# A third weight pair's first products at three seams, and TensorE orders that alternate row halves, in a two-layer decoder trunk

## The chip, the cores and the metric

The kernel runs on one core of a Trainium2 chip. The metric is device time in microseconds of one launch; the time before is the median of three runs, 2896.13 us (2890.81 to 2898.02). A core has five engines with an instruction queue each: TensorE (PE, matmuls into PSUM; its weight loads are listed as PEld), VectorE (DVE), ScalarE (ACT), GpSimd (POOL) and SyncE (SP, here the queue that issues most transfers).

## The reference

Two layers on a sequence of 1024 tokens of width 1024, in float32. Each layer adds three normed branches to the residual: a token mixer, cross-attention into 256 memory tokens, and an MLP with a squared ReLU:

```python
x = x + rms_norm(t, g[1])            # t: RG-LRU block in layer 0, RWKV-7 in layer 1
c = mem_cross_attention(rms_norm(x, g[2]), mem_n, c_w_q[i], c_w_kv[i], c_w_o[i])
x = x + rms_norm(c, g[3])
m = sqrelu_mlp(rms_norm(x, g[4]), m_w_up[i], m_w_down[i])
x = x + rms_norm(m, g[5])
```

RWKV-7 has 16 heads of 64 and a state of 64 x 64 per head:

```python
w_log = -softplus(-(w0 + tanh(xw @ w1) @ w2)) - 0.5        # decay, from a width of 64
a = sigmoid(a0 + (xa @ a1) @ a2)                           # also from a width of 64
state = state * w_t + (state a_t) b_t^T + v_t k_t^T        # per token and head
y_t = state r_t
bonus = sum(r * k * r_k, per head) * v
out = ((group_norm(y) + bonus) * g) @ w_o
```

## The kernel before, in words

**Products in three parts.** A float32 product is made of three fp32r matmuls: `split` (lines 228 to 235) gives a tile's rounded high part (a cast on ScalarE, L233) and the rest (a subtraction on VectorE, L234), and `mm3` (L314 to L320) issues high x high, high x low and low x high. A plain fp32 matmul, where it is used, shows as two records. Activations are stored transposed, 128 rows of the width by 512 tokens.

**Who sets the order.** The program is written once in Python; a planner with a model of the engines then puts the instructions of each engine in order. It takes the earliest written instruction that its model holds to be ready, so TensorE's order can differ from the written one. Tiles come from pools: 45 buffers of 4 KB per partition (`u`), and PSUM's 8 banks in two pools. `bank(n)` takes a bank from pool n. Two tools fix orders: `line(name)` puts each engine's instructions of a block behind the ones that the last block of that name gave to that engine, and `behind()` puts them behind the last instruction written so far. Weights come through a list recorded in a dry run: `fetch` loads entries ahead (`depth + ahead`), `advance` splits the next `depth` of them.

**The 7-product projections** (`cphase`, lines 466 to 563). A projection takes its weights in pairs of 128 columns, counted from 0, and makes each pair with seven half-size products (p1 to p7) in place of eight. A product is four steps of `mm3`, so 12 matmuls. p1 and p2 (in `begin`) need the activations' quarters b11 and b21, both from the first 512 tokens. p5, p6, p7 and p4 need t1 to t4, sums of quarters, and p3 needs b22; these come from the second 512 tokens, which `combine_in` (lines 373 to 432) transposes on TensorE (L386), scales (L389 on VectorE, L391 on ScalarE), subtracts (L417) and splits. `combine_w` forms a pair's weight sums on GpSimd.

**The seams.** Before a projection stands `tphase`, an output projection over eight tiles of 128 tokens; `tail` norms each tile (L655 to L663), stores the residual (L657) and loads the old one (L636). Three projections are begun while the one before still runs: the query projection of layer 1 behind RWKV and both MLP up-projections. There `make` (L454), called after token tiles 4 and 5, loads, splits and combines pairs 0 and 1. At the seam `together` begins both pairs (p1, p2 of pair 0, p1 of pair 1, then the second half's transposes, then p2 of pair 1), and goes on with p5, p6, p7, p3, p4 for both. Pair 2 comes after them: its `begin` is also what fetches its weights and those of the pairs behind it. The order of p1, p2 and the transposes on TensorE is the planner's.

**RWKV.** `decay(f)` (L1297) makes two tiles of 128 x 1024, the decay and the gate a, from operands of 64 rows: rows 0 to 63 for one, 64 to 127 for the other, each in two halves of 512 tokens, one after the other. `evac_v` (L1526) finishes the value projection for tile f: centring products (L1545), the bonus sum as an fp32 product with a matrix of ones (L1562), the gate product; then stores. The scan (L1737 to L1821) runs over 16 chunks of 64 tokens. Its steps stand in a list `todo`, each in `line("scan")`, so every engine runs them in the written order. `values`, `from_state`, `solved`, `update` and `output` are the recurrence for chunk c; `scan_gram` (L1644) makes chunk c+1's grams for half of the heads per call, 8 fp32 matmuls of 64 rows that alternate in the text between the row halves; `scan_keys` transposes keys, `scan_mask` masks grams; `flip_out` (L1698) transposes the finished chunk c-2 (L1703), multiplies on VectorE (L1708) and adds on GpSimd (L1709). `load` brings a pair of chunks' operands through SP.

Of the kernel before, what the change touches and what calls it, by code (L numbers as in the profile page):

```python
# [20 lines left out]
UP = (2, 2)  # L21
# [28 lines left out]
class Net:  # L50
# [322 lines left out]
    def combine_in(self, xs, hf, g, B):  # L373
# [4 lines left out]
        def turned(ks):  # L378
            for k in ks:
                if k % 2 == 0:  # L380
                    t = raw[hf, k // 2] = self.unit()
                    pair = [self.bank(1) for _ in range(2)] if hf else self.halves()
                o = slice((k % 2) * 512, (k % 2) * 512 + 512)
                p = pair[k % 2]
                for i, x in enumerate(xs):
                    nc.tensor.transpose(p[:, i * 128:i * 128 + 128], x[:, k * 128:k * 128 + 128], self.ident)  # L386
                gc = self.colt[:, g + k:g + k + 1]
                if k in (1, 3):
                    nc.vector.tensor_scalar(t[:, o], p, gc, None, ALU.mult)  # L389
                else:  # L390
                    nc.scalar.activation(t[:, o], p, AF.Copy, scale=gc)  # L391
# [62 lines left out]
    def make(self, w, i):  # L454

        self.depth, self.ahead = 0, 2 - 2 * i
        two, first = self.take(("w", w, i))
        self.made[i] = two, first, self.combine_w(two, first)
# [7 lines left out]
    def cphase(self, w, n, B, func, evac, then=None, ahead=2):  # L466
# [4 lines left out]


        place = lambda i: 0 if i < ahead else (i + 1) % 2

        def begin(i, mid=lambda: None):
            two, first = self.made[i][:2] if i in self.made else self.take(("w", w, i))
            h, l = first
            x, z = self.bank(place(i)), self.bank(place(i))
            c0, c1 = self.unit(), self.unit()
            self.product(x, (h[:, a], l[:, a]), B["b11"], True, False)  # L480
            nc.scalar.copy(c0[:, a], x)
            mid()
            self.product(z, (h[:, b], l[:, b]), B["b21"], True, True)
            nc.vector.tensor_add(c0[:, a], c0[:, a], z)
            st[i] = x, c0, c1, two, first
# [44 lines left out]

        def together(two, mid=lambda: None, late=lambda: None):
            for i in two:
                narrow(i)
                begin(i, mid if i == two[-1] else lambda: None)
                finish(i)
                if then and i == n - 2:
                    then[0]()
            late()
            for step in (p5, p6, p7, p3, p4):
                for i in two:  # L540
                    step(*st[i], i)
# [9 lines left out]

        together(range(ahead), second_half)
        for i in range(ahead, n - 2 if then else n):
            narrow(i)
            begin(i)
            finish(i)
            rest()
# [579 lines left out]
def rwkv_consts(self):  # L1137
# [37 lines left out]
    for h in range(2):  # L1175
        nc.gpsimd.memset(self.ones[h * 64:h * 64 + 64, h * 64:h * 64 + 64], 1.0)

    self.center = c([128, 128], "center")
    nc.vector.scalar_tensor_tensor(self.center, self.ones, -1.0 / 64, self.ident, ALU.mult, ALU.add)
# [61 lines left out]
def rwkv(self, X, xt, lw_wa, lw_g, post, mid):  # L1241
# [55 lines left out]
    def decay(f):  # L1297
        cs = slice(f * 128, f * 128 + 128)
        c1 = lambda t: t[:, f:f + 1]
        lw, a = self.unit(), self.unit()  # L1300
        for t, r, b in ((lw, slice(0, 64), self.w0h), (a, slice(64, 128), self.a0h)):
            for hf in range(2):
                s = slice(hf * 512, hf * 512 + 512)
                p = self.bank()
                self.mm3(p, (wa2[0][r, cs], wa2[1][r, cs]), (hwa[0][r, s], hwa[1][r, s]), True, True)
                nc.scalar.activation(t[:, s], p, AF.Tanh, bias=c1(b), scale=0.5)
# [219 lines left out]
    def evac_v(f, p):  # L1526
# [8 lines left out]
        pr, kp = ld.pop(f)  # L1535
        nc.vector.scalar_tensor_tensor(pr, pr, self.col("r_k", f), kp, ALU.mult, ALU.mult)


# [20 lines left out]
        for e in range(2):  # L1559
            s = slice(e * 512, e * 512 + 512)  # L1560
            bp = self.bank()
            mm(bp, self.ones, pr[:, s], start=True, stop=True)  # L1562
            nc.vector.tensor_mul(vt[:, s], vt[:, s], bp)
# [80 lines left out]
    def scan_gram(c, g):  # L1644
# [5 lines left out]
        for q in range(4):  # L1650
            for h in range(2):
                mm(s["pv", g][h][:, q, :], s["st"][g][hr[h], q].rearrange("p w t -> p (w t)"), s["mv"][hr[h], 4 * g + q],  # L1652
                   start=True, stop=True)

# [82 lines left out]
    for c in range(16):  # L1737
# [58 lines left out]
        if c:  # L1796
            todo += [(scan_scale, c + 1)]
        todo += [(values, 0), (from_state, 0)]
        if c > 1:
            todo += [(flip_out, c - 2)]  # L1800
        todo += [(values, 1), (from_state, 1)]
        if c:
            todo += [(post_var, c - 1)]
        todo += [(solved, 0), (solved, 1)]
        if c:
            todo += [(scan_gram, c + 1, 0)]
# [29 lines left out]
def network(net, I, out):  # L1836
# [12 lines left out]
    for l in range(2):  # L1849
        if l == 1:  # L1850
            xt = nxt
            post, nxt = net.tail(g(1, 1), x[3], x[4], net.lncol(1, 2), combine=True)
            rwkv(net, raw, xt, *early, post, lambda tt: tt in MAKE and net.make(I["c_w_q"][1], MAKE.index(tt)))
        post, xt = net.tail(g(l, 3), x[3 * l + 1], x[3 * l + 2], net.lncol(l, 4), combine=True)
        net.xattn(l, nxt, post, lambda tt: tt in MAKE and net.make(I["m_w_up"][l], MAKE.index(tt)))
        raw = []
# [26 lines left out]
```

## Time and profile before

| | us |
|---|---|
| median of 3 runs | 2896.13 (2890.81 to 2898.02) |
| the profiled execution | 2897.32 |
| its span | 2895.6 |
| TensorE busy | 2804.9 (97%) |
| VectorE busy | 1834.2 (63%) |
| ScalarE busy | 1421.7 (49%) |
| GpSimd busy | 907.3 (31%) |

The three seams lie near 690, 2043 and 2277 us of the span, the decays between 1359 and 1463, the value projections from 1636 to 1765, the scan from 1764 to 1935. Busy time of TensorE is read with care: matmuls overlap, one record covers about 0.39 us while the next starts 0.23 us after it, so a stretch can show 5.00 of 5 us busy and still be at half pace; the number of instructions in a stretch and the granted clock (PEclk) tell. In a timeline the first two columns are start and duration in us, equal neighbours are merged (x16), and the bracket gives idle time of the engine before and what ended it. In the stretches each engine has busy us and a count. In the list of waits stand total, times and the longest.

### The profile page before, as it was taken

How to read it: one execution, taken by the hardware profiler on the slowest of the kernel's cores; microseconds unless marked ns; L12 is line 12 of the kernel's file. 1: busy time of each engine (PE TensorE's matmuls, PEld its weight loads, DVE VectorE, ACT ScalarE, POOL GpSimd, SP SyncE). 2: the span in 40 equal slices, each digit the busy share in tenths (PEclk: the TensorE clock that was granted, in tenths of full speed). 3: DMA queues.
4: the chain of work that ended last, by engine and by line, in shares of the span. 5: the costliest groups of instructions: out<-in, count | busy, mean ns of one | idle time of the engine just before them, and what ended most of it. 6: DMA issues, size and time to landing. Idle time of an engine off the chain costs nothing.

```text
span 2895.6 us, 42717 instructions
## 1 busy us (share of the span) xinstructions
PE 2804.9 (97%) x16955; PEld 2341.9 (81%) x16955; DVE 1834.2 (63%) x1995; ACT 1421.7 (49%) x2195; POOL 907.3 (31%) x962
## 2 busy tenths in 40 slices
PE   7999999999999999999999999999999999999998
PEld 6888788887888888887877777888788788888886
DVE  5577566657455577886675724775665645567778
ACT  5455354546454543347561634564463645454333
POOL 2000114023666500012288113753202276650001
PEclk9999999999999999999999999999999999999999
DMA  8212342323444654442657898952232354464443
GB/s 260 73 50 74 109 161 74 111 80 96 154 148 156 224 183 155 151 136 83 172 142 210 224 231 237 231 146 88 88 95 73 109 163 154 138 243 162 151 175 116
DMA packets 383592, 421.92 MB, mean 146 GB/s; under 512 B 91184, under 2 KB 294176, under 8 KB 383392
## 3 DMA queue, kind: packets, MB, share of 16 engines
q1 hardware_dynamic: 371360, 379.19, 43.5%
q0 software_dynamic: 11568, 39.41, 3.8%
q8 instruction: 133, 2.18, 0.3%
q14 instruction: 67, 0.55, 0.1%
q10 hardware_dynamic: 464, 0.59, 0.1%
HBM read 283.79 MB, written 134.74 MB: 145 GB/s over the span
## 4 chain that ended last, share of the span: by engine, by line
PE 86%; DVE 5%; ACT 3%; DMA 2%; issue 2%; SPq 1%; POOL 0%; DVEq 0%; POOLq 0%; ACTq 0%
PE q L318 17%; PE q L320 17%; PE q L319 17%; PE p L318 9%; PE p L320 9%; PE p L319 9%; DVE u L234 1%; PE q L1652 1%; ACT u L233 1%; PE q L386 1%; DMA u<-in_b_w_rkv 1%; DVE u L1199 1%; PE q L1545 1%; PE q L1769 1%; ACT u L930 1%
## 5 line engine op out<-in xcount | busy, mean ns | idle before, releaser
L234 DVE TENSOR_TENSOR u<-u,u 128x1024 fp32r<-128x1024 f32 (+1 forms) x594 | 799.3, 1378 | 353.9 <-ACT u L233 331.8
L233 ACT CAST u<-u 128x1024 fp32r<-128x1024 f32 (+1 forms) x594 | 582.2, 1019 | 416.3 <-DVE u L1042 224.7
L318 PE MATMUL q<-u,u 128*128 128x512 f32 (+2 forms) x1984 | 760.3, 386 | 15.4 <-ACT u L391 10.0
L319 PE MATMUL q<-u,u 128*128 128x512 f32 (+2 forms) x1984 | 759.6, 384 | 0.5 <-POOL u L366 0.5
L320 PE MATMUL q<-u,u 128*128 128x512 f32 (+2 forms) x1984 | 753.9, 384 | 0.8 <-DVE u L234 0.8
L318 PE MATMUL p<-u,u 128*128 128x512 f32 (+1 forms) x1472 | 557.0, 381 | 12.2 <-ACT u L233 5.4
L319 PE MATMUL p<-u,u 128*128 128x512 f32 (+1 forms) x1472 | 553.1, 376 | 3.7 <-DVE u L234 3.6
L320 PE MATMUL p<-u,u 128*128 128x512 f32 (+1 forms) x1472 | 552.6, 376 | 3.6 <-DVE u L234 3.6
L318 PEld LDWEIGHTS q<-u,u 128*128 128x128 f32 (+1 forms) x1984 | 373.6, 189 | 92.8 <-ACT u L391 10.9
L320 PEld LDWEIGHTS q<-u,u 128*128 128x128 f32 (+1 forms) x1984 | 373.9, 189 | 74.3 <-DVE u L234 1.0
L329 POOL TENSOR_SCALAR s<-s 128x1 f32<-128x1 f32 x98 | 39.0, 398 | 1258.3 <-ACT u L327 1256.7
L319 PEld LDWEIGHTS q<-u,u 128*128 128x128 f32 (+1 forms) x1984 | 374.2, 189 | 72.3 <-POOL u L366 1.0
L318 PEld LDWEIGHTS p<-u,u 128*128 128x128 f32 x1472 | 281.2, 191 | 66.4 <-ACT u L233 7.5
L319 PEld LDWEIGHTS p<-u,u 128*128 128x128 f32 x1472 | 281.3, 191 | 55.0 <-DVE u L234 6.7
L320 PEld LDWEIGHTS p<-u,u 128*128 128x128 f32 x1472 | 281.3, 191 | 54.7 <-DVE u L234 5.2
L440 POOL TENSOR_TENSOR u<-u,u 128x512 f32<-128x512 f32 x120 | 189.1, 1579 | 9.0 <-PE q L319 5.1
L1100 DVE TENSOR_TENSOR z<-z,q 128x512 f32<-128x512 f32 x192 | 130.5, 683 | 81.0 <-PE q L320 81.0
L318 PE MATMUL q<-z,u 128*128 128x512 f32 x320 | 124.7, 391 | 1.6 <-ACT u L233 1.6
L320 PE MATMUL q<-z,u 128*128 128x512 f32 x320 | 124.5, 390 | 1.1 <-DVE u L234 1.1
L319 PE MATMUL q<-z,u 128*128 128x512 f32 x320 | 124.6, 389 | 0.0
L441 POOL TENSOR_TENSOR u<-u 128x512 f32<-128x512 f32 x40 | 70.0, 1749 | 166.1 <-DVE u L234 63.7
L997 POOL TENSOR_TENSOR u<-u,u 128x512 f32<-128x512 f32 x32 | 44.2, 1381 | 177.0 <-ACT u L986 159.8
(247 smaller groups left out, 3334.6 us busy)
## 6 DMA issues: line engine op xcount, KB each, us to landing
u<-d SPq DMA_DIRECT2D x194, 512.0 KB, 4.7
d<-u SPq DMA_DIRECT2D x109, 512.0 KB, 3.5
d<-u POOLq DMA_DIRECT2D x68, 512.0 KB, 3.3
d<-u SPq DMA_DIRECT2D x132, 256.0 KB, 3.6
u<-in_m_w_up SPq DMA_DIRECT2D x64, 512.0 KB, 5.5
u<-in_m_w_down SPq DMA_DIRECT2D x64, 512.0 KB, 8.1
u<-in_c_w_kv SPq DMA_DIRECT2D x32, 512.0 KB, 6.5
u<-in_b_w_rkv SPq DMA_DIRECT2D x24, 512.0 KB, 6.2
```

The costliest lines, as they stand in the source:

```text
L233: self.nc.scalar.copy(hv, src)
L234: (eng or self.nc.vector).tensor_tensor(lv, src, hv, ALU.subtract)
L318: mm(o, ah, bh, start=first, stop=False, **kw)
L319: mm(o, ah, bl, start=False, stop=False, **kw)
L320: mm(o, al, bh, start=False, stop=last, **kw)
L329: nc.gpsimd.tensor_scalar(v, ss, 1.0 / n, eps, ALU.mult, ALU.add)
L386: nc.tensor.transpose(p[:, i * 128:i * 128 + 128], x[:, k * 128:k * 128 + 128], self.ident)
L440: sub = lambda o, x, y: nc.gpsimd.tensor_tensor(o, x, y, ALU.subtract)
L441: nc.gpsimd.tensor_tensor(s[:, a], f1[:, a], f1[:, b], ALU.add)
L930: nc.scalar.activation(e[:, s], p[:, s], AF.Exp, bias=mx[:, i:i + 1], scale=1.0 / 16.0, accum_out=sm[:, i:i + 1])
L997: tt(s1, r21, r22, ALU.add)
L1100: nc.vector.tensor_add(to_, to_, o)
```

## The change

- `make` is called from token tile 4 on. For tiles 4 and 5 it looks ahead by two in both cases, so that tile 5 also asks for pair 2's weights; for tiles 6 and 7 it splits them.
- At the three seams pair 2's `begin` (p1, p2) moves into `together`, ahead of p5, and its `combine_w` ahead of p7. The transposes of the second half and p1, p2 of the three pairs form the line "seam": TensorE runs them in the written order. Where no pair was made early (the query projection of layer 0), nothing changes.
- `decay` takes both tiles' matmuls for a half of the tokens in turn, row half by row half, into two banks, in the line "decay"; `scan_gram`'s matmuls form the line "gram" inside the scan's.
- The bonus sum takes a split of r x k x r_k and an fp32r matrix of ones: two fp32r matmuls for one fp32 matmul.
- In the scan `flip_out` moves from between the two calls of `values` to behind `solved`.

```diff
@@ combine_in @@
-                for i, x in enumerate(xs):
-                    nc.tensor.transpose(p[:, i * 128:i * 128 + 128], x[:, k * 128:k * 128 + 128], self.ident)
+                with self.line("seam") if hf and self.held is None else ExitStack():
+                    for i, x in enumerate(xs):
+                        nc.tensor.transpose(p[:, i * 128:i * 128 + 128], x[:, k * 128:k * 128 + 128], self.ident)
@@ make @@
-        self.depth, self.ahead = 0, 2 - 2 * i
+        if i >= len(MAKE):
+            self.depth, self.ahead = 2, 0
+            self.fetch(self.taken - 1)
+            return
+        self.depth, self.ahead = 0, 2
@@ cphase @@
+        early = ahead if 0 in self.made else None
...
-            self.product(x, (h[:, a], l[:, a]), B["b11"], True, False)
+            seam = lambda: self.line("seam") if early and i <= early else ExitStack()
+            with seam():
+                self.product(x, (h[:, a], l[:, a]), B["b11"], True, False)
             nc.scalar.copy(c0[:, a], x)
             mid()
-            self.product(z, (h[:, b], l[:, b]), B["b21"], True, True)
+            with seam():
+                self.product(z, (h[:, b], l[:, b]), B["b21"], True, True)
...
+            if third:
+                self.depth, self.ahead = 0, 2
+                begin(third)
+                self.depth, self.ahead = UP
             late()
             for step in (p5, p6, p7, p3, p4):
+                if step is p7 and third:
+                    finish(third)
...
-        together(range(ahead), second_half)
+        together(range(ahead), second_half, third=early)
         for i in range(ahead, n - 2 if then else n):
             narrow(i)
-            begin(i)
-            finish(i)
+            if i == early:
+                self.fetch(self.taken - 1)
+            else:
+                begin(i)
+                finish(i)
@@ decay @@
-        for t, r, b in ((lw, slice(0, 64), self.w0h), (a, slice(64, 128), self.a0h)):
-            for hf in range(2):
-                s = slice(hf * 512, hf * 512 + 512)
-                p = self.bank()
-                self.mm3(p, (wa2[0][r, cs], wa2[1][r, cs]), (hwa[0][r, s], hwa[1][r, s]), True, True)
+        for hf in range(2):
+            s = slice(hf * 512, hf * 512 + 512)
+            ps = [self.bank() for _ in range(2)]
+            for n, (i, j) in enumerate(((0, 0), (0, 1), (1, 0))):
+                for p, r in zip(ps, hr):
+                    with self.line("decay"):
+                        mm(p, wa2[i][r, cs], hwa[j][r, s], start=n == 0, stop=n == 2)
+            for t, p, b in zip((lw, a), ps, (self.w0h, self.a0h)):
                 nc.scalar.activation(t[:, s], p, AF.Tanh, bias=c1(b), scale=0.5)
@@ evac_v @@
+        prs = self.split(pr)
...
-            mm(bp, self.ones, pr[:, s], start=True, stop=True)
+            for i in range(2):
+                mm(bp, self.ones_r, prs[i][:, s], start=i == 0, stop=i == 1)
@@ scan @@
-        todo += [(values, 0), (from_state, 0)]
-        if c > 1:
-            todo += [(flip_out, c - 2)]
-        todo += [(values, 1), (from_state, 1)]
+        todo += [(values, 0), (from_state, 0), (values, 1), (from_state, 1)]
         if c:
             todo += [(post_var, c - 1)]
         todo += [(solved, 0), (solved, 1)]
+        if c > 1:
+            todo += [(flip_out, c - 2)]
```

More of the change, by code (lines that the diff above doesn't have):

```diff
@@ L529, in narrow, with together @@
                 self.depth, self.ahead = 2 * (n - 1 - i), 0
-        def together(two, mid=lambda: None, late=lambda: None):
+        def together(two, mid=lambda: None, late=lambda: None, third=None):
             for i in two:
@@ L1176, in rwkv_consts @@
         nc.gpsimd.memset(self.ones[h * 64:h * 64 + 64, h * 64:h * 64 + 64], 1.0)
+    self.ones_r = self.cpool.tile([128, 128], F32R, name="ones_r", tag="ones_r")
+    nc.vector.tensor_copy(self.ones_r, self.ones)
     self.center = c([128, 128], "center")
@@ L1651, in scan_gram @@
             for h in range(2):
-                mm(s["pv", g][h][:, q, :], s["st"][g][hr[h], q].rearrange("p w t -> p (w t)"), s["mv"][hr[h], 4 * g + q],
-                   start=True, stop=True)
+                with self.line("gram"):
+                    mm(s["pv", g][h][:, q, :], s["st"][g][hr[h], q].rearrange("p w t -> p (w t)"), s["mv"][hr[h], 4 * g + q],
+                       start=True, stop=True)
     def scan_mask(c, g):
@@ L1852, in network @@
             post, nxt = net.tail(g(1, 1), x[3], x[4], net.lncol(1, 2), combine=True)
-            rwkv(net, raw, xt, *early, post, lambda tt: tt in MAKE and net.make(I["c_w_q"][1], MAKE.index(tt)))
+            rwkv(net, raw, xt, *early, post, lambda tt: tt >= MAKE[0] and net.make(I["c_w_q"][1], tt - MAKE[0]))
         post, xt = net.tail(g(l, 3), x[3 * l + 1], x[3 * l + 2], net.lncol(l, 4), combine=True)
-        net.xattn(l, nxt, post, lambda tt: tt in MAKE and net.make(I["m_w_up"][l], MAKE.index(tt)))
+        net.xattn(l, nxt, post, lambda tt: tt >= MAKE[0] and net.make(I["m_w_up"][l], tt - MAKE[0]))
         raw = []
```

## The prediction

> **What bounds the kernel now.** I read the page's table of engines first.
>
> ```profile
> span 2895.6 us, 42717 instructions
> PE 2804.9 (97%) x16955; PEld 2341.9 (81%) x16955; DVE 1834.2 (63%) x1995; ACT 1421.7 (49%) x2195; POOL 907.3 (31%) x962
> ...
> L234 DVE TENSOR_TENSOR u<-u,u 128x1024 fp32r<-128x1024 f32 (+1 forms) x594 | 799.3, 1378 | 353.9 <-ACT u L233 331.8
> L233 ACT CAST u<-u 128x1024 fp32r<-128x1024 f32 (+1 forms) x594 | 582.2, 1019 | 416.3 <-DVE u L1042 224.7
> ```
>
> TensorE is busy for 97% of the span, so time goes only where TensorE has less to do, does it denser, or waits less. The other engines matter where TensorE waits for them. The waits of TensorE, longest first, begin with this line:
>
> ```profile
> PE q L318 <- ACT u L391: 10.0, 3, 3.3
> ```
>
> Three waits of 3.3 us, all for the scaling copy of the second half's transposes (L391). They are the three seams. Next, stretches of time: one of plain products, the stretch behind each wait (from the last transpose's slot to the first product of pair 2), a piece of the second seam, and the stages of the other edits.
>
> ```profile
> core 0: us, PE busy (x) PEld busy (x) DVE busy (x) ACT busy (x) POOL busy (x), PEclk, DMA share, GB/s
> 800.00:900.00 100.00, 100.00 (x443) 82.84 (x442) 54.29 (x39) 47.34 (x62) 67.55 (x54) 1.00 0.47 150
> 691.10:723.93 32.83, 29.21 (x123) 23.62 (x121) 25.89 (x25) 23.29 (x28) 9.78 (x5) 0.95 0.40 112
> 2043.40:2076.98 33.58, 30.25 (x123) 24.64 (x121) 25.32 (x25) 16.94 (x21) 8.49 (x4) 0.90 0.23 63
> 2276.92:2309.36 32.44, 29.11 (x123) 23.77 (x121) 26.26 (x25) 23.39 (x28) 8.79 (x5) 0.95 0.41 114
> 2047.00:2052.00 5.00, 5.00 (x12) 3.94 (x13) 5.00 (x5) 4.67 (x6) 0.00 (x0) 0.50 0.42 105
> 1360.00:1470.00 110.00, 110.00 (x785) 88.66 (x786) 72.67 (x71) 70.84 (x94) 39.24 (x47) 0.98 0.57 159
> 1636.00:1760.00 124.00, 118.66 (x1120) 93.62 (x1119) 38.64 (x50) 44.84 (x63) 33.36 (x50) 0.97 0.87 230
> 1800.00:1900.00 100.00, 98.01 (x2040) 88.51 (x2037) 73.99 (x140) 57.94 (x248) 79.56 (x90) 1.00 1.04 231
> ```
>
> The first row gives the pace: 100 us hold about 441 products (443 less the tails at the edge), 0.227 us each. Behind each seam stand 120 products (five steps, two pairs, twelve matmuls), which at that pace are 27.2 us; the stretches are 32.8, 33.6 and 32.4 long. A seam thus loses 5.6, 6.3 and 5.2 us, 17.1 in all, though only 10.0 of it is idle: after the wait the granted clock is 0.50 for a while, and 5 us hold 12 products where 22 would fit.
>
> **Part 1, the seams.** The change puts pair 2's first two products, 24 matmuls or 24 x 0.227 = 5.4 us, between pair 1's second product and the first that waits (p5). It adds no product. If p5 then starts at full clock and on time, each seam gives back the smaller of 5.4 and its loss: 5.4 + 5.4 + 5.2 = 16. Whether p5 is on time is read from TensorE and VectorE at the first seam.
>
> ```profile
> 684.78 1.48 PE L386 MATMUL q<-ident,u 128*128 128x128 f32 x12
> ...
> 688.17 0.60 PE L386 MATMUL q<-ident,u 128*128 128x128 f32 x4
> ...
> 689.31 1.94 PE L386 MATMUL q<-ident,u 128*128 128x128 f32 x16
> 694.58 0.80 PE L318 MATMUL q<-u,u 128*128 128x512 f32 x1 [3.33 <-ACT u L391]
> ```
>
> ```profile
> 684.08 0.75 DVE L663 TENSOR_SCALAR u<-u,s 128x1024 f32<-128x1024 f32 x1 [0.39 <-POOL s L331]
> 688.59 1.41 DVE L389 TENSOR_SCALAR u<-q,colt 128x512 f32<-128x512 f32 x2 [3.76 <-PE q L386]
> ```
>
> The order on TensorE was twelve transposes, 9 of pair 1's products, the four of the last token tile, 3 products, 16 transposes. The fixed order makes all 32 transposes first. The last token tile is written at 684.08 + 0.75 = 684.83, and transposing starts at 684.78, so it is there in time. At 1.94 us for 16, the transposes end near 688.6, the 36 products behind them near 696.8. The operand t1 took from 688.17 to 694.58, 6.4 us; the four transposes that completed it come now near 686.5, so it is due near 693, 4 us before p5. p5 starts 2.2 us later than before but loses no 2.1 us to the clock, so the steps after it keep their times, and VectorE, which is full behind the seam (5.00 of 5), starts earlier.
>
> What else moves: pair 2's two weight loads and split go from behind the seam to token tiles 5 and 6. On SP the loads go ahead of the last tiles' residual loads (L636) and stores (L657). The split, 1.02 us on ScalarE and 1.38 on VectorE, lies ahead of the last tile's norm; at worst it delays L663 by 1.4 us per seam, 4.2 in all, if those queues are full just then. VectorE sat idle for 3.76 us before L389, so I take a third, 1 us in all. Pair 2's combination comes before p7: VectorE adds two splits and a half there, under 20 us of products. Seams: 15 us; between 10 (the idle time alone) and 17.
>
> [...]
>
> **Part 2, the decays.** One decay is 12 matmuls on 64 rows, in groups of six.
>
> ```profile
> 1411.35 0.50 PE L318 MATMUL q<-u,u 64*128 64x512 f32 x1
> ...
> 1412.94 0.51 PE L318 MATMUL p<-u,u 128*128 128x512 f32 x1
> ```
>
> ```profile
> 1371.61 0.49 PE L318 MATMUL q<-u,u 64*128 64x512 f32 x1
> 1371.95 0.39 PE L319 MATMUL q<-u,u 64*128 64x512 f32 x1
> 1372.18 0.39 PE L320 MATMUL q<-u,u 64*128 64x512 f32 x1
> 1372.19 0.62 PE L318 MATMUL q<-u,u 64*128 64x512 f32 x2
> ...
> 1373.77 0.50 PE L318 MATMUL p<-u,u 128*128 128x512 f32 x1
> ```
>
> Six alone take 1.59 us, 0.23 each and 0.2 for going in and out (the first step is 0.34). In the twelve, where the planner let the halves meet, matmuls of different halves start 0.01 us apart (1372.18 and 1372.19) and all take 2.16. So halves do run side by side. Alternating from the start, a group is three steps: 3 x 0.23 + 0.2 = 0.9 us, or 1.6 for a whole decay if its two groups are neighbours: 13 to 14.5 us for eight decays. Before, it is between 8 x 2.16 = 17.3 (all met) and 16 x 1.59 = 25.4 (all alone); the timeline has about half alone, so 21.5. The gain lies between 3 and 12; I take 7. TensorE is busy for 110 of 110 us here with VectorE and ScalarE at two thirds, so it is all on the path. The two banks now held at once come from a pool of four.
>
> **Part 3, the bonus sums.** An fp32 product with the ones becomes two fp32r products.
>
> ```profile
> 1761.50 1.02 PE L1562 MATMUL q<-u,ones 128*128 128x512 f32 x2
> ...
> 1763.06 1.02 PE L1562 MATMUL q<-u,ones 128*128 128x512 f32 x2
> ```
>
> From one to the next are 1.56 us with three gate products between (0.68): 0.88, against 2 x 0.227 = 0.45 in future. 16 times 0.43 is 6.9 us. The price is eight splits, 8 us of ScalarE and 11 of VectorE, in a stretch of 124 us where they are busy for 45 and 39; the product r x k that is split doesn't depend on the value projection and can be early. If it isn't, the split's 2.4 us stands ahead of the sum at the last tile. The new constant is one 128x128 copy on VectorE, once. Gain 6.4; between 3 and 7.
>
> **Part 4, the scan.** Grams alternate already for the first half of the heads, not for the second.
>
> ```profile
> 1850.74 1.16 PE L1652 MATMUL q<-z,u 64*128 64x128 f32 x16
> 1851.83 1.15 PE L1782 MATMUL q<-u,u 128*64 128x64 f32 x32
> 1852.92 1.09 PE L1676 MATMUL q<-ident,u 128*128 128x128 f32 x8
> 1853.94 1.71 PE L1652 MATMUL q<-z,u 64*128 64x128 f32 x16
> 1855.58 1.15 PE L1789 MATMUL q<-u,u 128*64 128x64 f32 x32
> ```
>
> ```profile
> 1852.57 1.77 DVE L1784 TENSOR_TENSOR u<-u,q 64x256 f32<-64x256 f32 x4 [0.74 <-PE q L1782]
> ```
>
> ```profile
> 1787.18 2.08 PE L1652 MATMUL q<-z,u 64*128 64x128 f32 x16 [3.73 <-issue]
> ```
>
> To the next row it is 1.09 us for the first and 1.64 for the second: 0.55 apiece, for 13 chunks and four grams ahead of the scan, at most 9.3. Not all comes through. The four ahead (2.2 us) end in front of the wait of 3.73 at 1787.18, where chunk 1 has caught up with the loads of its successor; they only lengthen it. In every second chunk the second row half's bank is the one that the state update's additions give back, at 1852.57 + 1.77 = 1854.34; in the fixed order it is asked for at 1853.94 at once, so 0.4 of the 0.55 turns into waiting. 7 x 0.15 + 6 x 0.45 = 4 us; between 0 and 7. The flip of the chunk before last adds nothing: its transposes go past the second values, state and solve products, its multiplication past the four of the solve into the 0.74 us in which VectorE waited for L1782, its addition on GpSimd behind the variance; no DMA goes with it.
>
> **The sum.** 15 + 7 + 6.4 + 4 = 32.4. The profiled execution took 2897.3 us, span 2895.6; it is 1.2 above the median of the three runs, 2896.1. 2896.1 - 32.4 = 2863.7, so 2864.
>
> **The rivals.** *The loads pace it from the value projections on.* The DMA share is 0.87 there and 1.04 in the scan, and the wait at 1787.18 is for a load. If the loads set the pace, parts 3 and 4 give nothing: 2896.1 - 22 = 2874. Against it: within the scan TensorE is busy for 98 of 100 us, so loads arrive in time there. [...]
>
> *Slower: the third pair's weights hold the fixed order.*
>
> ```profile
> 696.43 1.54 SPq L245 DMA_DIRECT2D u<-in_m_w_up  x2
> ```
>
> ```profile
> u<-in_m_w_up SPq DMA_DIRECT2D x64, 512.0 KB, 5.5
> ```
>
> Pair 2's loads were issued only at 696.43, 20 us after the last token tile's products, because buffers were short. If they get a buffer no sooner now, the weights are there at 697.97 + 5.5 and split 2.4 later, near 706. Pair 2's first product is due near 691.3 and everything behind it on TensorE waits: 14.5 us and the slow clock after. The delay decides from about 5.5 us on, where a seam gains nothing, and the kernel turns slower past some 11 us. At 14.5 + 2 a seam loses 11 net, three 33, the other parts give back 17.4: 2912. Against it: the 16 buffers of the output projection's rows come free during the last token tile, ahead of all this, and the load is asked for two tiles earlier.
>
> *The edits do little:* the planner places the rest of the kernel anew, losing some 25 us elsewhere: 2889. Nothing in the profile points to it.
>
> **How the numbers follow.** Forecast, all four parts at work: 0.74, with its own range 2853 to 2873. Loads as the pace: 0.15. Weights late in full: 0.05. Little: 0.06. The range 2852 to 2882 takes in the first two and the seams' lower bound (10), decays at 3 and bonus at 3 with no gain in the scan (16 in all: 2880). A measurement of this kernel can tell some 0.3% (9 us) from no change. Faster by more than that: the first two cases and a part of the last, 0.91. Within: 0.04. Slower: 0.05.
>
> **What would show it.** Right: no wait for L391 at the seams and no clock below 0.9 there; 120 + 24 products without a gap; decays of 0.9 per six; no L1562 matmul over 0.4; second grams near 1.2 us, a longer wait before the first gram of chunk 2. Wrong: a wait at L318 for weights (L233 or L234) in front of p5; the gap at chunk 2 longer by all that parts 3 and 4 gained.

## The result, and the profile after

The changed kernel takes 2872.55 us, the median of 6 runs (2869.12 to 2876.36); the kernel before, run beside it, 2897.07 us (2890.81 to 2906.06). The ratio is 0.9914, with a 95% interval of 0.9901 to 0.9928: faster by 24.5 us where 32.4 were forecast. The profiled execution took 2871.51 us, 25.8 less than that of before (2897.3). The median lies at the slow edge of the forecast's own range (2853 to 2873). The experiments show that the four terms did not miss together. The seams came out as worked out, the decays gave nothing in the end, the bonus sums lost part of their gain, and the scan's sum was reached by a step that was wrong.

The page's table of engines, for the changed kernel:

```profile
span 2869.8 us, 42738 instructions
PE 2779.0 (97%) x16955; PEld 2320.8 (81%) x16955; DVE 1845.2 (64%) x2004; ACT 1431.3 (50%) x2203; POOL 913.3 (32%) x962
```

TensorE's busy time fell from 2804.9 by 25.9 us with the same number of matmuls, and its idle time stayed at 91 us (span less busy time). So whatever waits the seams lost came back elsewhere, and what was won is that the same matmuls run denser or at a higher clock (0.993 on average, 0.987 before). The waits of TensorE that bear on the four parts:

```profile
PE q L1679 <- DMA u<-d: 5.5, 1, 5.5
...
PE q L1570 <- DVE u L1589: 2.8, 1, 2.8
...
PE q L387 <- DVE u L681: 2.2, 3, 0.9
PE p L318 <- DVE u L1350: 2.1, 1, 2.1
PE q L387 <- DVE u L390: 2.0, 3, 0.7
```

The three waits of 3.3 us for the scaling copy, ahead of p5, are gone from the list. In their place stand two short ones a seam inside the transposes (L387), 1.4 us together. New are a wait of 2.8 for a bonus multiplication (L1589), and 5.5 for the scan's load, which was 3.7. The waits for the r multiplication (L1519, L1495 before) grew from 1.3 to 5.6 us, three in number. TensorE at the first seam, with p5 in the last row:

```profile
685.81 2.95 PE L387 MATMUL q<-ident,u 128*128 128x128 f32 x25 [0.86 <-DVE u L681]
689.41 0.66 PE L387 MATMUL q<-ident,u 128*128 128x128 f32 x4 [0.65 <-DVE u L390]
...
698.10 0.39 PE L318 MATMUL q<-u,u 128*128 128x512 f32 x1
```

Now the stretches behind the seams:

```profile
core 0: us, PE busy (x) PEld busy (x) DVE busy (x) ACT busy (x) POOL busy (x), PEclk, DMA share, GB/s
691.00:724.00 33.00, 33.00 (x147) 27.31 (x147) 26.08 (x26) 23.02 (x29) 9.36 (x4) 1.00 0.27 72
2021.00:2054.00 33.00, 31.71 (x155) 26.57 (x155) 28.40 (x28) 21.30 (x27) 9.37 (x4) 1.00 0.12 33
```

The first row holds 147 matmuls in 33 us without a gap, at clock 1.00; before, 123 took 32.83 at 0.95.

To see where the time went, I took the start of the same instruction in the timeline of each kernel and subtracted it from its start before. The table shows this lead, in us. Only its changes from one row to the next mean something, and an execution can wander by itself by some us: the scan's part alone, in which TensorE has the same order as before up to there, came to the scan 4.7 us late.

| Landmark (start before) | changed | seams alone | decays alone | bonus alone | scan alone | grams without flip |
|---|---|---|---|---|---|---|
| transposes ahead of the first seam (662.1) | 0.3 | -0.6 | -0.5 | 0.2 | -0.7 | 0.0 |
| last transposes into RWKV (1336.6) | 5.5 | 4.6 | 0.0 | -1.5 | -2.4 | 0.8 |
| sixth gram (1493.8) | 9.3 | 4.6 | 4.3 | -1.7 | -4.2 | 0.6 |
| eighth gram (1551.3) | 5.4 | 5.1 | -8.0 | -1.6 | -6.4 | 0.5 |
| first value tile centred (1637.8) | 5.2 | 4.5 | -6.0 | 0.1 | -4.0 | 1.1 |
| second value tile centred (1643.2) | 2.2 | 4.5 | -6.0 | -0.7 | -4.0 | 1.2 |
| first gram of the scan (1764.7) | 10.3 | 5.5 | -2.4 | 3.1 | -4.7 | 0.5 |
| last output product (1933.8) | 14.2 | 5.9 | -5.7 | 2.5 | 1.4 | 1.2 |
| transposes ahead of the second seam (2014.5) | 16.6 | 7.0 | -5.5 | 3.2 | 3.8 | 2.3 |
| behind the second seam (2124.8) | 21.3 | 11.7 | -5.4 | 4.0 | 4.9 | 2.9 |
| last product (2882.8) | 25.8 | 16.2 | -5.4 | 4.0 | 4.5 | 2.9 |

In the changed kernel each seam gives about 5. The decays give 3.8 up to the sixth gram, and then 3.9 is lost by the eighth. Another 3.0 goes between the first two value tiles. The value projections and the scan bring the rest of what lies between the seams.

### The profile page after: what moved, and what is told of

Its sections match the earlier page's. It is cut to its first block, busy times and chain, and to the rows that moved or that the text cites. A ratio compares the mean times of both kernels' runs of the same rounds, so it can differ in the third digit from the quotient of the medians.

```text
span 2869.8 us, 42738 instructions
## 1 busy us (share of the span) xinstructions
PE 2779.0 (97%) x16955; PEld 2320.8 (81%) x16955; DVE 1845.2 (64%) x2004; ACT 1431.3 (50%) x2203; POOL 913.3 (32%) x962
## 4 chain that ended last, share of the span: by engine, by line
PE 81%; DVE 5%; POOL 3%; ACT 3%; DMA 3%; issue 3%; SPq 2%; ACTq 0%; DVEq 0%; POOLq 0%
PE q L318 17%; PE q L320 17%; PE q L319 17%; PE p L318 8%; PE p L320 8%; PE p L319 8%; PE q L1679 1%; DMA u<-d 1%; DVE u L234 1%; POOL u L1435 1%; ACT u L233 1%; DMA u<-in_b_w_rkv 1%; POOL w L1433 1%; PE q L1796 1%; ACT u L327 1%
## 5 line engine op out<-in xcount | busy, mean ns | idle before, releaser
L234 DVE TENSOR_TENSOR u<-u,u 128x1024 fp32r<-128x1024 f32 (+1 forms) x602 | 809.2, 1375 | 370.9 <-ACT u L233 342.2
L233 ACT CAST u<-u 128x1024 fp32r<-128x1024 f32 (+1 forms) x602 | 591.8, 1020 | 436.6 <-DVE u L1060 224.5
L318 PE MATMUL q<-u,u 128*128 128x512 f32 (+1 forms) x1952 | 744.2, 383 | 5.3 <-ACT u L233 2.4
L319 PE MATMUL q<-u,u 128*128 128x512 f32 (+1 forms) x1952 | 745.8, 382 | 0.5 <-POOL u L366 0.5
L320 PE MATMUL q<-u,u 128*128 128x512 f32 (+1 forms) x1952 | 740.4, 382 | 0.8 <-DVE u L234 0.8
L318 PEld LDWEIGHTS q<-u,u 128*128 128x128 f32 x1952 | 367.0, 188 | 77.3 <-ACT u L233 3.5
L320 PEld LDWEIGHTS q<-u,u 128*128 128x128 f32 x1952 | 366.9, 188 | 72.1 <-DVE u L234 1.0
L319 PEld LDWEIGHTS q<-u,u 128*128 128x128 f32 x1952 | 367.0, 188 | 71.6 <-POOL u L366 1.0
L442 POOL TENSOR_TENSOR u<-u 128x512 f32<-128x512 f32 x40 | 76.0, 1899 | 145.3 <-DVE u L234 73.1
```

Of the source, the lines that this page charges most:

```text
L233: self.nc.scalar.copy(hv, src)
L234: (eng or self.nc.vector).tensor_tensor(lv, src, hv, ALU.subtract)
L318: mm(o, ah, bh, start=first, stop=False, **kw)
L319: mm(o, ah, bl, start=False, stop=False, **kw)
L320: mm(o, al, bh, start=False, stop=last, **kw)
L442: nc.gpsimd.tensor_tensor(s[:, a], f1[:, a], f1[:, b], ALU.add)
```

## The experiments

Each part was first put alone into the kernel before. The medians of before in the three sets of runs were 2897.07, 2895.45 and 2894.22; each ratio is to those of its own set.

**The seams alone.** The hunks of the seams (fixed order, third pair, its early weights), nothing else.

> Before plus the seam part alone: the fixed order of transposes and early products, the third pair's two products ahead of p5, its weights taken by the call after the last MAKE entry. Theory (the seams gave what was forecast, and the shortfall lies in RWKV alone): 14.4 us, 4.8 a seam, so 2896 - 14.4 = 2882 and a ratio of 0.9950; the waits for the scaling copy are gone. Rival (the changed kernel's landmarks credit the seams with time that other parts saved, because all parts move each other): under 10 or over 18 us.

Measured: 2882.30 us, ratio 0.9956 (0.9940 to 0.9972): 14.8 us by the medians, 12.7 (8 to 17) by the ratio. From landmark to landmark the three seams give 5.2, 4.7 and 4.5, in sum 14.4, as in the changed kernel. The theory holds. (The next expectation's "12.7 us by the medians" is the figure by the ratio.)

**The fixed order left out.** The seams alone, without the line that holds TensorE's order:

```
-                with self.line("seam") if hf and self.held is None else ExitStack():
+                with ExitStack():
...
-            seam = lambda: self.line("seam") if early and i <= early else ExitStack()
+            seam = ExitStack
```

> Before plus the seam part, but without the fixed order: the third pair's two products are still asked for ahead of p5 and its weights two token tiles earlier, and the planner may place transposes and early products as it likes. The seam part whole gave 12.7 us by the medians and 14.4 by the landmarks of its trace. Theory (the early products are what fills the wait, and without the order the planner spreads the last sixteen transposes and puts other products ahead, so that the operand of p5 comes late again): half of it, 5 to 9 us, 2887 to 2891, with waits for the scaling copy back in part. Rival (24 products more ahead of p5 cover 3.3 us whatever the order of the transposes): 12 to 15 us, 2881 to 2884. Other rival (the order alone does it, the products only move): 0 to 3 us.

Measured: 2894.84 us, ratio 1.0003 (0.9994 to 1.0012): no gain, where the theory had half of it and the first rival all of it. It lies in the range of the other rival, that the order alone does it. Its TensorE waits, and its timeline at the first seam:

```profile
PE q L318 <- ACT u L392: 9.2, 3, 3.1
```

```profile
684.58 1.47 PE L387 MATMUL q<-ident,u 128*128 128x128 f32 x12
...
688.66 0.60 PE L387 MATMUL q<-ident,u 128*128 128x128 f32 x4
689.78 2.09 PE L387 MATMUL q<-ident,u 128*128 128x128 f32 x16 [0.51 <-ACT u L392]
694.93 0.80 PE L318 MATMUL q<-z,u 128*128 128x512 f32 x1 [3.06 <-ACT u L392]
```

This is nearly the order of before again: twelve transposes, products, four, sixteen, and then p5 waits 3.06 us with nothing in front of it. The planner did not put the early products ahead of p5; being asked for early in the program was not enough here, and without the order the 24 products bring nothing. What the order brings without the products was not run, so how the gain divides between the two stays open.

**The decays alone.**

> Before plus the alternating decays alone. Theory (the decays do become shorter, by about 4 us up to the fourth gram, but the k projections' end and the change to r are bound by VectorE and its mixes, which take TensorE's lead back): the eight decays read 18 us instead of 21.6 in the trace, the time falls by 0 to 2 us only, 2895. Rival (the decays' 4 us come through, and the loss behind them belongs to another part): 4 us, 2892. Forecast as it was: 7 us, 2889.

Measured: 2902.27 us, ratio 1.0025 (1.0014 to 1.0036): slower, by 5.2 us by the medians and 7 by the ratio, and outside all three forecasts. The table's column shows how: 4.3 won up to the sixth gram, 12.4 lost up to the eighth. TensorE, ScalarE and SP at that place, each from its own timeline:

```profile
1489.41 2.08 PE L1384 MATMUL q<-u,u 64*64 64x64 f32 x64
1501.27 0.77 PE L318 MATMUL p<-u,u 128*128 128x512 f32 x1 [9.77 <-DVE u L1329]
```

```profile
1481.86 2.08 ACT L1424 COPY u<-u 64x1024 f32<-64x1024 f32 x1 [12.58 <-POOL u L1414]
...
1491.06 1.04 ACT L233 CAST u<-u 128x1024 fp32r<-128x1024 f32 x1 [6.16 <-DMA u<-in_b_w_rkv]
```

```profile
1481.86 0.34 SPq L1425 DMA_DIRECT2D d<-u  x1
1483.97 0.48 SPq L1426 DMA_DIRECT2D d<-u  x1
1484.55 2.21 SPq L249 DMA_DIRECT2D u<-in_b_w_rkv  x2
```

Read it from the bottom up. On SP two weight loads (L249) stand behind the stores of the first solve (L1425, L1426), and these wait for GpSimd, which ends the solve just ahead of 1481.86. That is 0.6 us earlier than before (1482.50 for the copy), where TensorE is 4.3 us ahead. ScalarE's copy of the solve (L1424) has idled 12.58 us for the same end, and the cast behind it (L233) idles 6.16 more for the weight load. Behind that cast stand the r mixes, and on VectorE the multiplication (L1329) that gives back the k products' banks. TensorE waits 9.77 us for it. In the kernel before, the planner had put one of the two loads ahead of the store:

```profile
1475.68 1.23 SPq L249 DMA_DIRECT2D u<-in_b_w_rkv  x1
1483.11 0.56 SPq L1422 DMA_DIRECT2D d<-u  x1
```

**The solve's store one step later.** To test this, one number moves the copy and stores of the first solve behind the last two k projections. It was done to the kernel before, to the decays alone, and to the changed kernel.

```
-SL, SO, ST = (2, 5, 8, 9), (2, 5, 8, 9), (5, 8, 12, 13)
+SL, SO, ST = (2, 5, 8, 9), (2, 5, 8, 9), (6, 8, 12, 13)
```

> The kernel before with the alternating decays and that number changed. The decays alone gave 2902. Theory (the wait of 9.8 us at the change from k to r comes from a weight load and a cast that stand behind the solve's store; with the store moved behind them both the loss of 12 us goes and the decays' 4 us come through): 3 to 4 us faster than the kernel before with the number alone changed, 2888 to 2890. Rival (the decays' order of banks and weights itself disturbs the k projections, wherever the store stands): still slower than that kernel, 2897 or more.

> The kernel before with the same one number changed, and nothing else. Theory (the copy's wait holds up the kernel before too, by its gaps of 2.1 and 1.5 us between the sixth and the eighth gram and the slow clock behind them): 3 to 5 us faster than before, 2892 to 2894. Rival (VectorE's own work): the same, 2896.

Measured: with the decays 2892.55 us, ratio 0.9991 (0.9982 to 1.0000), 9.7 us less than the decays alone and far outside their interval. Without them 2895.44, ratio 0.9998 (0.9987 to 1.0009): the kernel before gains nothing, against the theory. With the decays the lead stays: 4.6 at the sixth gram, 4.6 at the eighth, 4.4 at the first value tile, 4.5 at the scan, 3.8 at the end. So with the store moved the decays are worth some 4 us by the landmarks and 2.9 by the medians (against the kernel before with the store moved, theory: 3 to 4), and what took them was the order behind the solve.

**Which of the two queues.** In the decays alone, the copy of the first solve was given to GpSimd. Of its two stores the first, which doesn't need the copy, stayed on SP right behind the end of the solve (L1425, at 1482.97), and the weight loads behind it (L249, at 1483.41).

```
-        nc.scalar.copy(L[0:64].rearrange(...), xt_[0:64].rearrange(...))
+        (nc.scalar.copy if q else nc.gpsimd.tensor_copy)(L[0:64].rearrange(...), xt_[0:64].rearrange(...))
```

> The kernel before with the alternating decays, and the first solve's copy made by GpSimd, which computes the solve, instead of ScalarE; its store stays where it was on SP. The decays alone gave 2902, with the whole copy and store one step later 2892.6. ScalarE's queue is free here, but on SP the weight load that the second k product of the last pair needs still stands behind the solve's store. Theory (this load is the cause: issued at the end of the solve, cast after it lands, and in ScalarE's queue the r mixes behind that cast): most of the loss stays, 2898 to 2901. Rival (ScalarE's wait for the copy is the cause): the loss goes, 2891 to 2893.

Measured: 2915.39 us, ratio 1.0070 (1.0054 to 1.0086), slower than either theory said. ScalarE's timeline shows both reasons:

```profile
1489.29 1.05 ACT L233 CAST u<-u 128x1024 fp32r<-128x1024 f32 x1 [18.81 <-DMA u<-in_b_w_rkv]
...
1558.41 1.04 ACT L233 CAST u<-u 128x1024 fp32r<-128x1024 f32 x1 [33.05 <-DMA u<-in_b_w_rkv]
```

The first row answers the question. With no copy in its queue ScalarE still idles until the weight load lands, and TensorE waits 6.41 us instead of 9.77; of the 12.4 lost between the sixth and the eighth gram, 8.1 remains. So about two thirds of the loss is there without ScalarE's wait for the copy, with the load behind the store on SP. The second row is the same trap a second time: the planner put GpSimd's copy behind the next solve, at 1548.03, so the second store came to SP only at 1550.08, with another weight load behind it at 1551.20, and 18 us more were lost.

**The changed kernel without the decays.** Everything but the hunk of the decays.

> The changed kernel with the decays as before: two rows of six on one row half each. The decays alone made the kernel before 0.25% slower: they gained 4.3 us on TensorE and lost 12.4 at the change from the k to the r projections. Theory A (the decays are worth nothing anywhere, since GpSimd's first solve ends at the same time with or without them and ScalarE waits for its copy ahead of the r mixes): the same time as the changed kernel, 2871 to 2874. Theory B (the decays are a loss also here): 2866 to 2868, faster than the changed kernel by 4 to 7. Theory C (in the whole change they bring their 4 us and only alone they set off a bad order of a load behind the solve's store): 2875 to 2877.

Measured: 2871.99 us, ratio 0.9919 (0.9904 to 0.9934), against 2872.55 and 0.9914. In the whole change the decays bring no time that can be measured, as theory A has it; the other three parts make 23.5 us by the medians, near the sum of what each gave alone (14.8 + 3.5 + 4.0).

**The changed kernel with the store one step later.**

> The changed kernel with one number changed: the copy and stores of the first solve's result (solve_store of the first quarter) come one step later, behind the last two k projections instead of ahead of them, so that ScalarE's and SP's queues no longer stand behind GpSimd's solve there. Theory (that copy, for which ScalarE idles 11.3 us, is what took back TensorE's lead: r mixes, weight splits and the operands that free the k products' banks all stand behind it): the two waits of TensorE at the change from k to r go, 4 to 7 us come, 2865 to 2868. Rival (VectorE is full there by its own work, 20 of 20 us, and would be full wherever the copy stands): within 1.5 us of the changed kernel, 2870 to 2873. Rival on the other side: the later store delays the merges and the r projections wait for them, slower by 2 or more.

Measured: 2869.82 us, ratio 0.9912 (0.9898 to 0.9927). The median lies between the theory's range and the first rival's, and the intervals overlap, so the time doesn't tell it from the changed kernel. Its trace does: the wait for the k products' banks (2.1) is gone, and the lead goes from 6.9 at the sixth gram to 7.2 at the seventh, where the changed kernel fell from 9.3 to 6.9. But VectorE is still full from 1490 to 1510 (20.00 of 20 us) in both, and in this kernel the decays won only 2.3 up to the sixth gram instead of 3.8. So most of what is no longer lost there had not been won. A second loss stays in both: between the seventh and the eighth gram the lead falls by 1.5, behind a wait of 1.2 us for the r multiplication (L1519) and a clock of 0.50 (from 1519.67 to 1523.09 in the changed kernel).

**The bonus sums alone.**

> Before plus the bonus sums in two fp32r products alone. Theory (the sums are worth their full 6.4 us; what is missing was lost ahead of the value projections): 6 us, 2890. Rival (the splits hold VectorE and ScalarE at the change from r to v and cost a part): 3 to 4 us, 2892 to 2893. Second rival (the scan's first load sets when the scan starts, the load wait before the first gram of chunk 2 grows by what was gained): under 2 us.

Measured: 2893.61 us, ratio 0.9989 (0.9978 to 0.9999), 3.5 us by the medians (0.3 to 6.4 by the interval): the first rival, by the median. From the eighth gram to the scan its lead grows by 4.7, not 6.4. What is missing shows in the changed kernel too, on TensorE and VectorE at the first two value tiles:

```profile
1632.62 2.05 PE L1570 MATMUL q<-center,u 128*128 128x128 f32 x16 [0.42 <-ACT u L1553]
1635.55 0.50 PE L1588 MATMUL q<-u,ones_r 128*128 128x512 f32 x1 [0.88 <-ACT u L233]
...
1641.07 1.13 PE L1570 MATMUL q<-center,u 128*128 128x128 f32 x8 [2.84 <-DVE u L1589]
```

```profile
1636.67 1.28 DVE L1560 SCALAR_TENSOR_TENSOR u<-u,colt,u 128x1024 f32<-128x1024 f32 x1
1639.04 1.28 DVE L1560 SCALAR_TENSOR_TENSOR u<-u,colt,u 128x1024 f32<-128x1024 f32 x1 [1.09 <-DMA u<-d]
1640.24 1.28 DVE L1589 TENSOR_TENSOR u<-u,q 128x512 f32<-128x512 f32 x2
```

The first tile's split comes late (0.88 us). Then the r x k products of the second and third tile (L1560) stand in VectorE's queue ahead of the first tile's bonus multiplication (L1589), and the third waits for a load. TensorE needs the bank that L1589 gives back, and waits 2.84 us.

**VectorE's order there.** The changed kernel with the later store, and these operations held in program order:

```
+        with self.line("bonus"):
+            nc.vector.scalar_tensor_tensor(pr, pr, self.col("r_k", f), kp, ALU.mult, ALU.mult)
...
+            with self.line("bonus"):
+                nc.vector.tensor_mul(vt[:, s], vt[:, s], bp)
```

> The changed kernel with the first solve's store one step later (2869.8) and VectorE's order fixed for two operations: a tile's product of r and k ahead of its bonus multiplication, and the next tile's product behind it. Theory (the splits of the bonus products make the planner put the r x k product of the third tile, which waits for a load, ahead of the first tile's bonus multiplication, and TensorE waits 2.3 us for the bank that this gives back): the wait between the first and second tile's centring goes, 2 to 3 us, 2867 to 2868. Rival (VectorE is late there anyway, with the last solve and the mixes): the wait stays and the time is the same within 1 us, 2869 to 2871.

Measured: 2867.80 us, ratio 0.9904 (0.9887 to 0.9921). The wait is gone:

```profile
1635.06 0.97 PE L1589 MATMUL q<-u,ones_r 128*128 128x512 f32 x3
1636.91 2.05 PE L1571 MATMUL q<-center,u 128*128 128x128 f32 x16 [0.18 <-ACT u L1553]
```

From the first tile to the second the lead falls by 0.4, in the same kernel without this order by 2.5, so the mechanism is shown for this wait. It is the lowest median of all, 4.8 us under the changed kernel, but in another set of runs and with overlapping intervals; that it is faster is likely and not shown.

**The scan's part alone, and its grams without the flip.** First the whole part, then only the line that fixes the grams' order:

```
+                with self.line("gram"):
+                    mm(s["pv", g][h][:, q, :], ...)
```

> Before plus the scan's part alone: alternating grams for the second half of the heads, and the flip of the chunk before last behind the solve. Theory (0.15 to 0.45 per chunk come through as forecast, and the first grams ahead of the wait only lengthen it): 4 us, 2892. Rival (what the changed kernel gains behind the scan, 2.1 us in the last chunk and 2.3 at the change to the next stage, belongs to the scan's part too): 6 to 8 us, 2889.

> Before plus the alternating order of the second half's grams alone, the flip left where it was. The scan's part whole gave 4.0 us by the medians. Theory (the grams are the gain, the flip makes room for no more than 0.5): 3 to 4 us, 2892 to 2893. Rival (the state update gives back the second row half's bank only after the flip's work on VectorE, so without the flip's move the grams wait for their bank): 0 to 2 us, 2894 to 2896, with a wait of TensorE at the second grams of every second chunk.

Measured: the whole part 2893.04 us, ratio 0.9985 (0.9976 to 0.9995), 4.0 us by the medians (1.4 to 7.0 by the interval), the theory's size. By the landmarks it is more: the lead grows by 6.1 in the scan and by 2.4 behind it, 8.5 in sum, which is nearer the rival, in an execution that came to the scan 4.7 late. The runs don't settle which. The grams alone 2896.27, ratio 1.0002 (0.9993 to 1.0011): nothing. That expectation's theory falls, and its rival had the size right but not the place. TensorE's waits from 1800 to 1925, the grams alone first, then the whole part:

```profile
PE q L1704 <- DVE u L1697: 5.1, 9, 0.7
```

```profile
PE q L1783 <- issue: 1.4, 1, 1.4
```

Nine waits of 0.6 us for L1697 are new (in the kernel before they made 0.9 us in all). L1704 are the flip's transposes, which stood between the two value products, and L1697 the VectorE multiplication that makes their input. TensorE gets there half a microsecond sooner, VectorE doesn't, and the gain of each second gram is spent there. Moved behind the solve, the flip finds its input ready. The flip's move without the grams' order was not run, so how much of the gain it makes by itself stays open.

## Why the prediction was right and where it was wrong

| Term | forecast | changed kernel, by landmarks | alone, by medians |
|---|---|---|---|
| seams | 15 | 5.3 + 4.7 + 4.5 = 14.5 | 14.8 |
| decays | 7 | 3.8, then -4.1 up to the value tiles | slower by 5.2 |
| bonus sums | 6.4 | 5.2 up to the scan | 3.5 |
| scan | 4 | 3.9, and 2.3 behind it | 4.0 |
| sum | 32.4 | 25.5, with 0.3 ahead of the first seam 25.8 | |

The last column does not add up to the whole, since the decays alone set off an order that the whole change does not have. By the landmarks the shortfall is the decays' term, all 7 us of it. The bonus sums' shortfall and the 2.3 us behind the scan, which no term had, about cancel; that part of the agreement is luck.

**The seams** came out by the working: the waits of 3.3 us are gone, the clock stays at 1.00 (691 to 724, 2021 to 2054, 2249 to 2282 us), and p5 starts without a wait. Two things came out otherwise. The transposes wait 1.4 us a seam, so that p5 starts at 698.10 and not near 696.8: 2.2 us in all for the last tile's norm (L681), for which the prediction took 1, and 2.0 for VectorE's scaling copy (L390), which it did not have. And without the order the products gave nothing, which the prediction did not say. The rival of late weights did not occur; both loads were issued at 648.38, far ahead of the seam.

**The decays** are the step that failed, at the sentence "TensorE is busy for 110 of 110 us here with VectorE and ScalarE at two thirds, so it is all on the path". First the size. Where six matmuls stand together they take 0.90 us, as forecast:

```profile
1365.83 0.50 PE L1328 MATMUL q<-u,u 64*128 64x512 f32 x1
1366.26 0.50 PE L318 MATMUL p<-u,u 128*128 128x512 f32 x1
...
1366.91 1.65 PE L1328 MATMUL q<-u,u 64*128 64x512 f32 x11
...
1387.42 0.97 PE L1328 MATMUL q<-u,u 64*128 64x512 f32 x6
1388.32 0.50 PE L318 MATMUL p<-u,u 128*128 128x512 f32 x1
...
1432.21 0.50 PE L1328 MATMUL q<-u,u 64*128 64x512 f32 x1
1433.58 0.74 PE L1328 MATMUL q<-u,u 64*128 64x512 f32 x4 [0.87 <-DVE u L1406]
```

But six times in the stage the planner puts one matmul by itself among products (at 1365.83, 0.43 to the next row), and once the second bank is late (1432.21 to 1433.58, 1.37 us). The eight decays take about 17.9 us, not 14.5. Second the path: the window ended at 1470. Behind it TensorE's lead is not its own, because ScalarE and SP stand behind GpSimd's solve, which came only 0.6 us earlier with the decays alone. In the changed kernel ScalarE idles 11.26 us for it (11.47 before):

```profile
1476.62 2.06 ACT L1445 COPY u<-u 64x1024 f32<-64x1024 f32 x1 [11.26 <-POOL u L1435]
```

This copy starts 5.9 us earlier than before (1482.50), about as much as the first seam gave. TensorE came with a lead of 9.3 and left with 5.4. That the store's place takes the decays' gain is shown by the decays alone with and without the later store. That it does so in the changed kernel is shown only as far as the seventh gram, and 1.5 of the 3.9 us goes behind it, at the wait for L1519; why the kernel without the decays then reaches the first value tile 1.1 us earlier stays open.

**The bonus sums** had the right size, 0.45 for two matmuls, and a price that stood at the wrong tile and was larger. The prediction put the split's 2.4 us ahead of the sum "at the last tile"; it stands at the first, as 0.88 for the split and 2.84 for VectorE's order behind it. That leaves 3.2 of the 6.9 us. Of the 5.2 in the table some 1.7, by estimate, is not the sums but half of 3.4 us: the clock is at 0.50 for 3.4 us in this stretch (from 1721.06), before for 6.8 (from 1725.11). The decays alone, with the old sums, gain 3.6 there too.

**The scan** came out at the forecast's 4 us by the medians and at 6.3 by the landmarks, but a step was wrong: "The flip of the chunk before last adds nothing". The flip's move cost nothing, as meant, but the sum gave the grams their gain without it, and without it they gain nothing. The 2.3 us behind the scan go with the clock: in the kernel before it is at 0.50 from 1933.32 to 1940.14, in the changed kernel it stays at 1.00 there (1915 to 1930). Two other steps held: the four grams ahead of the scan only lengthen the wait for the load (3.73 to 5.54 us), and in every second chunk the second gram waits for its bank, 1.67 us against 1.16:

```profile
1842.16 1.67 PE L1679 MATMUL q<-z,u 64*128 64x128 f32 x16
...
1851.87 1.16 PE L1679 MATMUL q<-z,u 64*128 64x128 f32 x16
```

Of the rivals, the loads as the pace had 2874, nearer to the measured 2872.55 than the forecast's 2864, but not by its mechanism: the bonus sums and the scan bring time although the load's wait grows by 1.8. The planner's loss of some 25 us did not occur in the whole change, but in the decays alone its kind did, with 12 us.

## What to carry to other kernels

A stage in which TensorE is busy for every microsecond is still not proof that a gain there reaches the end (of the decays' 110 busy us 3.8 were won, and 3.9 were lost by the eighth gram): follow the lead to the next place where another engine's chain (here GpSimd's solve) releases a copy or a store, and read what stands behind that instruction on ScalarE's queue and on SP's. When one engine gets faster inside a loop, look at each short step between its parts whose input another engine makes; here the gain came only when the flip's transposes were moved away from theirs. Where a planner orders the instructions, check in the trace that an operation asked for early is early; at the seams it was so only with its order held.

## What the runs showed of the hardware

In the changed kernel the clock fell to 0.50 after 1.18 us of idle time, where the seams before had idled 3.3 us, and at another place it stayed at 1.00 after 2.84 us. TensorE's timeline at the first place:

```profile
1515.01 1.84 PE L1383 MATMUL q<-ind,u 128*128 128x2 f32 x16
1516.78 1.14 PE L1405 MATMUL q<-u,u 64*64 64x64 f32 x30
1519.10 0.47 PE L318 MATMUL p<-u,u 128*128 128x512 f32 x1 [1.18 <-DVE u L1519]
...
1520.03 0.63 PE L318 MATMUL p<-u,u 128*128 128x512 f32 x1
1520.46 0.63 PE L319 MATMUL p<-u,u 128*128 128x512 f32 x1
```

After a wait of only 1.18 us, with 3 us of very small products ahead of it (2 columns, then 64 x 64), the products go at 0.43 us instead of 0.23 (clock 0.50 from 1519.67 to 1523.09); after 2.84 us at 1641.07, with products of 512 columns ahead, the centring products go on at full pace (8 in 1.13 us, clock 1.00). The kernel before shows the clock halve with no wait at all, around such small products. First TensorE's timeline, then two stretches:

```profile
1443.61 1.72 PE L1359 MATMUL q<-ind,u 128*128 128x2 f32 x14
```

```profile
core 0: us, PE busy (x), PEclk, DMA share, GB/s
1441.80:1445.21 3.41, 3.41 (x23) 1.00 0.69 97
1445.21:1448.62 3.41, 3.41 (x51) 0.50 0.90 295
```

So here a stretch that the profile counts as busy for 3.41 of 3.41 us stands ahead of one at 0.50. That the products of 2 columns are the reason is a guess and not shown; no run changes them alone. At the three seams before, the stretches at 0.50 last 3.41, 6.83 and 3.41 us. The idle time just ahead doesn't tell the two places of the changed kernel apart: in the 3.41 us ahead of the halving at 1519.67 TensorE idles 1.18 us, and from 1639.14 to 1642.56, after which the clock stays at 1.00, 1.93 us.
